# First attention of a three-block transformer: values as hi beside lo in one stationary operand, two products and a fold, and the queries' transposes at the head of a step

## The chip, the core and the metric

The kernel runs on one core of a Trainium2 chip. The core has five engines, each with its own queue that is worked off in order: TensorE (PE in the profile; its loads of the stationary operand are PEld), VectorE (DVE), ScalarE (ACT), GpSimd (POOL) and SyncE (SP), which only issues DMA transfers here. The metric is the device time of one execution in microseconds (us); lower is better. The times given are medians of a few runs.

## What is computed

Two small models run one after the other on a sequence of 256 tokens of width 1024. The first has two layers, of which the first is attention with 16 query heads of 64 in 4 key groups, over 256 context tokens and 256 own tokens; the second is a neighbourhood attention. The second model has two layers of attention, one dense feed-forward and one mixture of experts. All is float32. What matters here is the attention of the very first layer:

```python
def gqa_axial_mixer(hx, hc, w_in, q_g, k_g, w_out, cos, sin, need_ctx_out):
    px = hx @ w_in
    ...
    k_all = jnp.concatenate([kc, k], axis=1)
    v_all = jnp.concatenate([vc, v], axis=1)
    ...
    def block(qi):
        s = jnp.einsum('bqkgd,bskd->bkgqs', qi, k_all).astype(jnp.float32) * ATTN_SCALE
        p = jax.nn.softmax(s, axis=-1).astype(v_all.dtype)
        return jnp.einsum('bkgqs,bskd->bqkgd', p, v_all)

    o = lax.map(block, qb)
    o = o.transpose(1, 0, 2, 3, 4, 5).reshape(b, t, A_WIDTH)
    yx = (o * jax.nn.silu(z)) @ w_out
    ...
    sc = jnp.einsum('bqkgd,bskd->bkgqs', qc, kc).astype(jnp.float32) * ATTN_SCALE
    pc = jax.nn.softmax(sc, axis=-1).astype(vc.dtype)
    oc = jnp.einsum('bkgqs,bskd->bqkgd', pc, vc).reshape(b, lc, A_WIDTH)
    yc = (oc * jax.nn.silu(zc)) @ w_out
```

The own tokens look at all 512 keys, the context tokens at the 256 context keys.

## The kernel before, in words

TensorE multiplies a reduced-precision float type (fp32r). To come near float32, each operand is kept as two such numbers, hi (the rounded value) and lo (the rest), and a product is three matmuls into the same PSUM bank: hi by hi, hi by lo and lo by hi (`mm3`).

The first attention is worked off in 32 units: 4 key groups, in each the two sequences (own tokens with nk = 512 keys, then context with nk = 256), in each two tiles of 128 queries, and in each two pairs of heads (`pr` 0 and 1). `pipeline` runs steps i = -3 to 35; in step i it calls each stage of `stages0` for the unit that the stage's lag names, in the order of that list. This list is the only thing that sets the order, for every engine's queue is filled in the order in which the code is written. In step i the list holds, in this order: `pv` of unit i-4 (products of the weights with the values), `turn` of unit i-3 (transposes of the weights `e`), the normalisation of unit i-2 on GpSimd (`norm0`, `norm1`, after a reciprocal on VectorE), between them `back` of unit i-3 (the transposed weights `pt`: hi copied by ScalarE, lo by VectorE), `out` of unit i-4, `scores` of unit i, `soft` of unit i-1 (exponentials on ScalarE), `q_turn` of unit i+2, `peak` of unit i (maximum and its scaling on VectorE), `q_split` of unit i+3 and `fill`.

`q_split` and `q_turn` do something only for units of even number, since two units share a set of queries. `q_split` makes hi (ScalarE) and lo (GpSimd) of four heads beside each other in `qn`; it therefore falls into odd steps. `q_turn` transposes these four on TensorE into a PSUM bank and ScalarE copies them out (`qs`); it falls into even steps. The transposes of queries, of weights and of the modulation row share two PSUM banks (`tp`), which are given out in turn.

`fill` gives TensorE other work in each step. With r = i mod 8: for r = 0 to 3 two pieces of a modulation vector (products of 32x512, `wf` with `sc`), for r = 4 to 7 a quarter of the next group's gate projection (12 products of 128x512, `hh`, `hl` with `wh`, `wl`), and from step 28 on a part of the output projection. So one period of eight steps is one key group.

Values are held as `vd[0]` (hi) and `vd[1]` (lo), each with its 64 columns twice, so that a product with the values gives the same 64 rows twice, in partitions 0 to 63 and 64 to 127 of the bank `o` (of which there is one). `pv` does `mm3` for each tile of 128 keys, three matmuls with a moving operand of 256 columns (two heads of 128 queries). `out` then multiplies, per head, one half of the partitions by the gate z and 0.5 on VectorE (line 151, 64x128, into z itself), casts the result to `og` hi on VectorE (line 141, 128x128), and GpSimd makes `og` lo (line 144). The gate tile z is `zb` in the rows, the maximum and sums are `sm`, the scores `s`.

Lines in the profile are often those of small helpers: 130 `mm`, 138 `acopy`, 141 `vcopy`, 144 `tt`, 148 `ts`, 151 `stt`, 154 `gscale`, 160 `act`; 704 are the transposes of `q_turn`, 738 those of `turn`, 322 the modulation's products, 836 the maximum, 847 the reciprocal.

Of the kernel before, what the change touches and what calls it, by code (L numbers as in the profile page):

```python
# [7 lines left out]
F = mybir.dt.float32  # L8
R = mybir.dt.float32r
ACTF = mybir.ActivationFunctionType  # L10
ALU = mybir.AluOpType
# [89 lines left out]
def tile_net(  # L101
# [4 lines left out]
    nc = tc.nc  # L106
    ctx.enter_context(tc.manual_schedule())

    def pool(name, side="left", bufs=1, space=None):
        kw = {} if space is None else {"space": space}  # L110
        if space is None:
            kw["side"] = side
        return tc.tile_pool(name=name, bufs=bufs, reuse_waits="tile", **kw)
# [13 lines left out]
    def mm(o, l, r, start, stop, rows=None):  # L127

        pos = {} if rows is None else {"tile_position": (rows, 0)}
        nc.tensor.matmul(o, l, r, start=start, stop=stop, **pos)  # L130

    def mm3(o, l, r, start, stop, rows=None):
        mm(o, l[0], r[0], start, False, rows)
        mm(o, l[0], r[1], False, False, rows)
        mm(o, l[1], r[0], False, stop, rows)

    def acopy(o, i):
        nc.scalar.copy(out=o, in_=i)  # L138

    def vcopy(o, i):  # L140
        nc.vector.tensor_copy(out=o, in_=i)

    def tt(o, a, b, op, eng=None):
        (eng or nc.vector).tensor_tensor(out=o, in0=a, in1=b, op=op)  # L144
# [5 lines left out]
    def stt(o, a, s, b, op0, op1, eng=None):  # L150
        (eng or nc.vector).scalar_tensor_tensor(out=o, in0=a, scalar=s, in1=b, op0=op0, op1=op1)  # L151

    def gscale(o, i, s):
        nc.gpsimd.tensor_scalar(out=o, in0=i, scalar1=s, scalar2=1.0, op0=ALU.mult, op1=ALU.mult)  # L154

    def gsub_lo(lo, src, hi):
        tt(lo, src, hi.bitcast(F), ALU.subtract, nc.gpsimd)

    def act(o, i, f, **kw):
        nc.scalar.activation(out=o, in_=i, func=f, **kw)  # L160
# [85 lines left out]
    p0 = L0.enter_context(pool("l0"))  # L246
# [48 lines left out]
    def bank(tag="mm"):  # L295
        return (pmm if tag == "mm" else ptp).tile([128, 512], F, tag=tag, name=tag)
# [10 lines left out]
    p = bank("tp")  # L307
# [41 lines left out]
    for s, dst in ((0, xT), (1, cT)):  # L349
        for t in range(2):  # L350
            for half in range(2):
                ps = bank("tp")
# [3 lines left out]
                o = dst[:, 4 * half:4 * half + 4, t * 128:(t + 1) * 128]  # L356
                i = ps.rearrange("p (k n) -> p k n", k=4)
# [129 lines left out]
    def group_N(key, hh, hl, nt, ahead=0):  # L487


        pss = [bank() for _ in range(nt)]  # L490
        w = [ws.get(key) for _ in range(ahead)]
        if ahead:
            yield pss
        for ch in range(4):
            wh, wl = w.pop(0) if w else ws.get(key)
            for t in range(nt):
                sl = slice(t * 128, (t + 1) * 128)
                for k in range(2):
                    kt = 2 * ch + k
                    mm3(pss[t], (hh[:, kt, sl], hl[:, kt, sl]), (wh[:, k, :], wl[:, k, :]), kt == 0, kt == 7)  # L500
                yield pss
# [10 lines left out]

    qf = p0.tile([128, 4, D], F, name="qf")
    kk2 = [p0.tile([128, 4, 512], R, name=f"kk{i}") for i in range(2)]
    vd = [p0.tile([128, 4, 4, 2, 64], R, name=f"vd{i}") for i in range(2)]
    nm = Norm([xT, cT])
    for kt in range(KT):
        nm.add(kt)
# [32 lines left out]
    p = bank("tp")  # L551
# [50 lines left out]
    def heads(a):  # L602
        return a.rearrange("p (h d) -> p h d", d=64)
# [57 lines left out]
    def keys_split(t):  # L661

        src = heads(kf[:, t, :]).unsqueeze(2).to_broadcast([128, 4, 2, 64])
        kn[t] = [prope.tile([128, 4, 2, 64], R, tag=f"kn{i}", name=f"kn{i}", bufs=2) for i in range(2)]
        acopy(kn[t][0], src)
        tt(kn[t][1], src, kn[t][0].bitcast(F), ALU.subtract)

    def keys_turn(t):

        kp = (t + 2) % 4  # L670
        for part in range(2):
            ps = bank("tp")
            for g in range(4):
                nc.tensor.transpose(ps[:, g * 128:(g + 1) * 128],
                                    kn[t][part][:, g].rearrange("p a d -> p (a d)").bitcast(F), ident)
            acopy(kk2[part][:, :, kp * 128:(kp + 1) * 128], ps.rearrange("p (g n) -> p g n", g=4))
# [7 lines left out]
    class Unit0:  # L684
# [64 lines left out]
        def pv(self):  # L749
            nkt = self.nk // 128  # L750
            self.o = o = pop.tile([128, 2, 128], F, tag="o", name="o")
            for k in range(nkt):
                vt = (k + 2) % 4
                mm3(o.rearrange("p h n -> p (h n)"), [vd[i][:, vt, self.g].rearrange("p a d -> p (a d)") for i in range(2)],
                    [self.pt[i][:, k].rearrange("p h n -> p (h n)") for i in range(2)], k == 0, k == nkt - 1)

        def out(self):
            g, tok = self.g, slice(self.tt_ * 128, (self.tt_ + 1) * 128)
            z = zb[g][:, self.pr, tok]
            for h in range(2):  # L760
                sl = slice(h * 64, h * 64 + 64)
                stt(z[sl], self.o[sl, h, :], 0.5, z[sl], ALU.mult, ALU.mult)
            vcopy(og[g][0][:, self.pr, tok], z)
            gsub_lo(og[g][1][:, self.pr, tok], z, og[g][0][:, self.pr, tok])

# [7 lines left out]
    def l0_done(j, t, ps):  # L773
        if j == 0:
            acopy(kf[:, t, :], ps[:, 0:256])
            vsrc = heads(ps[:, 256:512]).unsqueeze(2).to_broadcast([128, 4, 2, 64])
            acopy(vd[0][:, t], vsrc)
            tt(vd[1][:, t], vsrc, vd[0][:, t].bitcast(F), ALU.subtract)
        else:
            acopy(qf[:, t, (j - 1) * 512:j * 512], ps)  # L780
        r = ropes[j]
        r.squares(t, ps)
        if j == 2 and t:
            if t >= 2:
                r.turn(t - 2)
            r.gain(t - 1)
            if t == 3:
                r.gain(3)
        if t == 3:
            roots, *rest = r.pieces(j == 2)  # L790
            if j == 0:
                for t_ in range(4):
                    rest.append(lambda t_=t_: keys_split(t_))
                    if t_:
                        rest.append(lambda t_=t_: keys_turn(t_ - 1))
                rest.append(lambda: keys_turn(3))
            if j == 1:
                for n in range(1):
                    rest += [units[2 * n].q_split, units[2 * n].q_turn]
            later[0:0] = [roots]  # L800
            later.extend(rest)

    proj_N("l0in", 3, hh, hl, 4, l0_done, 3, begun)

    def z_tile(g):
# [20 lines left out]
    pa = A0.enter_context(pool("att0", bufs=2))  # L826
# [18 lines left out]
    def soft_norm(st_, e, nk, h, on_act=False):  # L845
# [4 lines left out]
        else:  # L850
            gscale(e[:, h, 0:nk], e[:, h, 0:nk], st_[:, 3, h:h + 1])

    def pipeline(units, stages, fill=None):

        lags = [lag for f, lag in stages if f != "fill"]
        for i in range(min(0, min(lags)), len(units) + max(lags)):
            for f, lag in stages:
                if f == "fill":
                    fill(i + lag)
                elif 0 <= i - lag < len(units):  # L860
                    getattr(units[i - lag], f)()

    stages0 = (("pv", 4), ("turn", 3), ("norm0", 2), ("back", 3), ("norm1", 2), ("out", 4), ("scores", 0), ("soft", 1),
               ("q_turn", -2), ("peak", 0), ("q_split", -3), ("fill", 0))

    def mods():
        for a, b in ((0, 2), (1, 1), (1, 0), (1, 2)):
# [42 lines left out]
    def fill(i):  # L910


        if i == 28:
            for _ in mod:
                pass
        if i in {27: 1, 29: 2, 33: 3}:
            ws.split_to(ws.base + {27: 1, 29: 2, 33: 3}[i], nc.gpsimd)
        for a in out_steps.get(i, ()):
            out_step(*a)
        if i < 0 or i >= 28:  # L920
            return
        g, r = i // 8 + 1, i % 8
        if r < 4:
            next(mod)
            next(mod)
            if r == 3 and g < 4:
                zw["a"] = ws.get("l0z")
        elif g < 4:
            if r == 4:
                next(mod)  # L930
                zw["b"] = ws.get("l0z")
                zb[g] = z_tile(g)
            z_step(g, 2 * (r - 4))
            z_step(g, 2 * (r - 4) + 1)
        if i == 25:
            H.close()
            og.append([O.enter_context(pool("og3", "right")).tile([128, 2, 512], R, name=f"og3{i}") for i in range(2)])
# [130 lines left out]
    pa = A1.enter_context(pool("att1", "right", bufs=2))  # L1068
# [524 lines left out]
    for n in range(len(steps) + 1):  # L1593
        if n < len(steps):
            e, f = steps[n]
# [3 lines left out]
        if n:  # L1599
            e, f = steps[n - 1]  # L1600
# [214 lines left out]
    ps = bank("tp")  # L1815
# [155 lines left out]
    for n in range(len(steps) + 1):  # L1971
        if n < len(steps):
            e, f = steps[n]
# [11 lines left out]
        if n:  # L1985
            e, f = steps[n - 1]
# [62 lines left out]
    for t in range(2):  # L2049
        for d in range(2):  # L2050
            sl = slice(d * 512, d * 512 + 512)
# [86 lines left out]
```

## Time and profile before

| | us |
|---|---|
| median of 3 runs | 2044.96 (2042.16 to 2048.12) |
| the profiled execution | 2042.53 |
| its span, first to last instruction | 2040.8 |
| TensorE busy | 1957.9 (96%) |
| VectorE busy | 1601.8 (78%) |
| ScalarE busy | 1311.4 (64%) |
| GpSimd busy | 279.3 (14%) |

The first attention lies between about 126 and 288 us of the span. The busy times are sums over stages with different limits. A window gives each engine's busy time in a stretch; a row of the timeline is a run of like instructions on one engine, with its start, its length and, in brackets, how long the engine stood idle before it and what ended that. Matmuls overlap, so the distance between the starts of two rows tells more on TensorE than a row's length.

### The profile page before, as it was taken

To read this page: it belongs to the slowest core of one execution; us is meant where nothing else is said; L and a number is where in the kernel's file an instruction comes from. 1 tells how busy PE (TensorE), PEld (TensorE's weight loads), DVE (VectorE), ACT (ScalarE), POOL (GpSimd) and SP (SyncE) were. 2 spreads that over 40 slices of the span, in tenths; PEclk is the share of its full clock that TensorE was granted. 3 is DMA by queue.
4 is the path that set the end of the run, shared out by engine and by line. 5 is a ranking of instruction groups with operands and counts; after the bars stand their busy time and mean duration, and the time that the engine had idled before them with its cause. 6 is when DMAs were issued, how large, how long until landed. Compare 5 with 4: busy or idle time off the path is not lost. (4 is left out here: it accounts for less than half of the span.)

```text
span 2040.8 us, 29700 instructions
## 1 busy us (share of the span) xinstructions
PE 1957.9 (96%) x11046; PEld 1660.0 (81%) x11046; DVE 1601.8 (78%) x2100; ACT 1311.4 (64%) x1877; POOL 279.3 (14%) x365
## 2 busy tenths in 40 slices
PE   7999988999899899999989999999999999999997
PEld 3777777888888799998978888788878888788885
DVE  4676766358569876657779999999989999899997
ACT  3555543347657544445668777778777777777775
POOL 2123430005414311103420000000000000000000
PEclk9999998999999999999989999999999999999999
DMA  8333422444253256567659999899999999999990
GB/s 289 94 135 104 157 82 83 119 132 91 83 173 104 73 178 194 181 203 264 238 198 365 377 369 375 312 375 364 364 366 328 368 364 372 333 357 370 368 365 22
DMA packets 270327, 494.38 MB, mean 242 GB/s; under 512 B 22834, under 2 KB 108042, under 8 KB 270176
## 3 DMA queue, kind: packets, MB, share of 16 engines
q1 hardware_dynamic: 269312, 490.91, 69.0%
q8 instruction: 89, 1.46, 0.3%
q0 software_dynamic: 544, 0.98, 0.2%
q10 hardware_dynamic: 320, 0.53, 0.1%
q14 instruction: 62, 0.51, 0.1%
HBM read 491.29 MB, written 1.08 MB: 241 GB/s over the span
## 5 line engine op out<-in xcount | busy, mean ns | idle before, releaser
L86 DVE TENSOR_TENSOR wl<-w,wh 128x1024 fp32r<-128x1024 f32 x624 | 752.2, 1226 | 58.5 <-ACT wh L85 21.6
L85 ACT CAST wh<-w 128x1024 fp32r<-128x1024 f32 x626 | 652.6, 1052 | 144.1 <-PE mm L130 104.5
L130 PE MATMUL mm<-wh,X 128*128 128x512 f32 x1792 | 573.4, 393 | 0.0
L130 PEld LDWEIGHTS mm<-wh,X 128*128 128x128 f32 x1792 | 337.2, 188 | 69.2
L86 DVE TENSOR_TENSOR wl<-wf,wh 128x1024 fp32r<-128x1024 f32 x190 | 238.4, 1265 | 173.2 <-ACT wh L85 171.6
L130 PE MATMUL mm<-wl,X 128*128 128x512 f32 x896 | 349.5, 390 | 0.0
L85 ACT CAST wh<-wf 128x1024 fp32r<-128x1024 f32 x200 | 206.4, 1040 | 156.2 <-PE mm L130 131.6
L130 PE MATMUL y<-wh,hid 128*128 128x512 f32 x896 | 287.0, 390 | 0.7 <-ACT hid L138 0.7
L130 PEld LDWEIGHTS y<-wh,hid 128*128 128x128 f32 x896 | 168.1, 188 | 35.9 <-ACT hid L138 0.9
L130 PEld LDWEIGHTS mm<-wl,X 128*128 128x128 f32 x896 | 168.7, 188 | 33.7
L130 PE MATMUL y<-wl,hid 128*128 128x512 f32 x448 | 174.4, 389 | 0.0
L130 PE MATMUL mm<-hh,wh 128*128 128x256 f32 (+1 forms) x432 | 125.9, 292 | 5.1 <-ACT wh L85 3.2
L130 PE MATMUL mm<-hh,wl 128*128 128x256 f32 (+1 forms) x432 | 125.4, 290 | 1.4 <-DVE wl L86 1.3
L130 PE MATMUL mm<-hl,wh 128*128 128x256 f32 (+1 forms) x432 | 125.2, 290 | 0.0
L130 PEld LDWEIGHTS y<-wl,hid 128*128 128x128 f32 x448 | 84.1, 188 | 17.1
L130 PEld LDWEIGHTS mm<-hh,wh 128*128 128x128 f32 x432 | 83.2, 193 | 7.0 <-ACT wh L85 4.3
L130 PEld LDWEIGHTS mm<-hh,wl 128*128 128x128 f32 x432 | 83.2, 193 | 2.5 <-DVE wl L86 1.9
L154 POOL TENSOR_SCALAR e<-e,sm 128x512 f32<-128x512 f32 (+2 forms) x112 | 66.9, 608 | 124.7 <-DVE sm L847 114.4
L130 PEld LDWEIGHTS mm<-hl,wh 128*128 128x128 f32 x432 | 83.2, 193 | 0.6
L130 PE MATMUL fill<-hh,wh 128*128 128x256 f32 (+1 forms) x240 | 75.0, 313 | 1.2 <-DVE ev L144 0.7
L144 DVE TENSOR_TENSOR pt<-tp,pt 128x512 fp32r<-128x512 f32 (+2 forms) x80 | 41.5, 552 | 41.2 <-ACT pt L138 41.2
L160 ACT ACTIVATE e<-s,sm 128x512 f32<-128x512 f32 (+2 forms) x128 | 71.8, 571 | 2.4 <-DVE sm L148 1.5
(351 smaller groups left out, 3438.9 us busy)
## 6 DMA issues: line engine op xcount, KB each, us to landing
w<-in_e_w_dram SPq DMA_DIRECT2D x313, 1024.0 KB, 7.1
wf<-in_w_dram SPq DMA_DIRECT2D x64, 512.0 KB, 4.6
wf<-in_w_mod_dram SPq DMA_DIRECT2D x48, 512.0 KB, 4.6
wf<-in_w_qkv_dram SPq DMA_DIRECT2D x48, 512.0 KB, 4.6
xT<-in_e_w_dram SPq DMA_DIRECT2D x23, 1024.0 KB, 7.1
wf<-in_b_w_in_dram SPq DMA_DIRECT2D x32, 512.0 KB, 3.8
wf<-in_a_w_in_dram SPq DMA_DIRECT2D x20, 512.0 KB, 3.7
wf<-in_w_o_dram SPq DMA_DIRECT2D x16, 512.0 KB, 3.4
```

What stands on the lines that cost most here:

```text
L85: nc.scalar.copy(out=hi[:, 0:m], in_=src)
L86: (low or nc.vector).tensor_tensor(out=lo[:, 0:m], in0=src, in1=hi[:, 0:m].bitcast(F), op=ALU.subtract)
L130: nc.tensor.matmul(o, l, r, start=start, stop=stop, **pos)
L144: (eng or nc.vector).tensor_tensor(out=o, in0=a, in1=b, op=op)
L154: nc.gpsimd.tensor_scalar(out=o, in0=i, scalar1=s, scalar2=1.0, op0=ALU.mult, op1=ALU.mult)
L160: nc.scalar.activation(out=o, in_=i, func=f, **kw)
```

## The change

Three things are changed, all in the first attention.

The values lie in one tile `vd`: in each group 64 columns of hi and beside them 64 columns of lo. `pv` does two matmuls for a tile of keys (`mm2`): this operand with the weights' hi and with their lo. Partitions 0 to 63 of `o` then hold the hi part, 64 to 127 the lo part; the product of lo with lo comes in addition to the three of before.

A new function `fold` adds the two: ScalarE copies partitions 64 to 127 with a factor of 0.5 into `fu`, and VectorE multiplies partitions 0 to 63 by 0.5 and adds `fu`, once for each head, into the two halves of `ft`. `out` then multiplies by z on GpSimd, and the cast and the low part follow as before.

`q_turn` moves from behind `soft` to the head of the list of stages.

```diff
+    def mm2(o, l, r, start, stop):
+
+        mm(o, l, r[0], start, False)
+        mm(o, l, r[1], False, stop)
...
-    vd = [p0.tile([128, 4, 4, 2, 64], R, name=f"vd{i}") for i in range(2)]
+    vd = p0.tile([128, 4, 4, 2, 64], R, name="vd")
...
-                mm3(o.rearrange("p h n -> p (h n)"), [vd[i][:, vt, self.g].rearrange("p a d -> p (a d)") for i in range(2)],
+                mm2(o.rearrange("p h n -> p (h n)"), vd[:, vt, self.g].rearrange("p a d -> p (a d)"),
                     [self.pt[i][:, k].rearrange("p h n -> p (h n)") for i in range(2)], k == 0, k == nkt - 1)
...
-            for h in range(2):
-                sl = slice(h * 64, h * 64 + 64)
-                stt(z[sl], self.o[sl, h, :], 0.5, z[sl], ALU.mult, ALU.mult)
+            t = fold(self.o, 128)
+            tt(z, t, z, ALU.mult, nc.gpsimd)
             vcopy(og[g][0][:, self.pr, tok], z)
             gsub_lo(og[g][1][:, self.pr, tok], z, og[g][0][:, self.pr, tok])
...
-            vsrc = heads(ps[:, 256:512]).unsqueeze(2).to_broadcast([128, 4, 2, 64])
-            acopy(vd[0][:, t], vsrc)
-            tt(vd[1][:, t], vsrc, vd[0][:, t].bitcast(F), ALU.subtract)
+            vsrc = heads(ps[:, 256:512])
+            acopy(vd[:, t, :, 0, :], vsrc)
+            tt(vd[:, t, :, 1, :], vsrc, vd[:, t, :, 0, :].bitcast(F), ALU.subtract)
...
+    def fold(o, n):
+
+        u = pa.tile([64, 2, n], F, tag="fu", name="fu", bufs=2)
+        t = pa.tile([128, n], F, tag="ft", name="ft", bufs=2)
+        act(u, o[64:128], ACTF.Copy, scale=0.5)
+        for h in range(2):
+            stt(t[h * 64:h * 64 + 64], o[0:64, h, :], 0.5, u[:, h, :], ALU.mult, ALU.add)
+        return t
...
-    stages0 = (("pv", 4), ("turn", 3), ("norm0", 2), ("back", 3), ("norm1", 2), ("out", 4), ("scores", 0), ("soft", 1),
-               ("q_turn", -2), ("peak", 0), ("q_split", -3), ("fill", 0))
+    stages0 = (("q_turn", -2), ("pv", 4), ("turn", 3), ("norm0", 2), ("back", 3), ("norm1", 2), ("out", 4), ("scores", 0),
+               ("soft", 1), ("peak", 0), ("q_split", -3), ("fill", 0))
```

How the queues change is seen at two places. The first is TensorE's queue in step 18, an even step with modulation in its fill (`o` are the products with the values, `e` the weights, `s` the scores, `qn` the queries). Before:

```order
L130 MATMUL o<-pt_1566,vd_205 128x256
L130 MATMUL o<-pt_1567,vd_205 128x256
L130 MATMUL o<-pt_1566,vd_206 128x256
...
L738 MATMUL tp<-cs,e 128x128 x4
L130 MATMUL s_1625<-kk_203,qs 128x512
...
L704 MATMUL tp<-cs,qn 128x128 x4
L322 MATMUL fill<-wf,sc_141 32x512 x4
```

After, from the end of step 17 on:

```order
L327 MATMUL fill<-wf,sc_141 32x512 x4
L709 MATMUL tp<-cs,qn 128x128 x4
L130 MATMUL o<-pt_1565,vd 128x256
L130 MATMUL o<-pt_1566,vd 128x256
...
L743 MATMUL tp<-cs,e 128x128 x4
L130 MATMUL s_1637<-kk_203,qs 128x512
```

The transposes of queries stand right behind the fill of step 17 now, ahead of the products of step 18. Of these, left out above in part, there are four instead of six, two for each of two tiles of keys.

The second place is step 17, an odd one, on VectorE and on GpSimd, with what each instruction waits for (`ft` and `fu` are the fold's tiles, `og` the gated output, `zb` the gate). VectorE before:

```order
L144 TENSOR_TENSOR pt_1567<-tp,pt_1566 128x2x128 [waits Activation_49] x2
L151 SCALAR_TENSOR_TENSOR zb<-o,zb 64x128 x2
L141 CAST og_240<-zb 128x128 [waits DVE_49]
L836 TENSOR_REDUCE sm<-s_1577 128x2 [waits PE_49,Pool_49]
L148 TENSOR_SCALAR sm<-sm 128x2 [waits DVE_49]
```

VectorE after:

```order
L149 TENSOR_TENSOR pt_1566<-tp,pt_1565 128x2x128 [waits Activation_49] x2
L156 SCALAR_TENSOR_TENSOR ft<-o,fu 64x128 [waits Activation_49]
L156 SCALAR_TENSOR_TENSOR ft<-o,fu 64x128
L146 CAST og_239<-zb 128x128 [waits Pool_49]
L840 TENSOR_REDUCE sm<-s_1580 128x2 [waits PE_49]
```

GpSimd before, step 17 and the first instruction of step 18:

```order
L154 TENSOR_SCALAR e<-e,sm 128x256 [waits DVE_49,PE_49]
L154 TENSOR_SCALAR e<-e,sm 128x256 [waits Activation_49]
L144 TENSOR_TENSOR og_241<-zb,og_240 128x128 [waits DVE_49]
L144 TENSOR_TENSOR qn<-qf,qn 128x4x64 [waits PE_49,Activation_49]
L154 TENSOR_SCALAR e<-e,sm 128x512 [waits DVE_49]
```

GpSimd after:

```order
L159 TENSOR_SCALAR e<-e,sm 128x256 [waits DVE_49,PE_49]
L159 TENSOR_SCALAR e<-e,sm 128x256 [waits Activation_49]
L149 TENSOR_TENSOR zb<-ft,zb 128x128 [waits DVE_49]
L149 TENSOR_TENSOR og_240<-zb,og_239 128x128 [waits DVE_49]
L149 TENSOR_TENSOR qn<-qf,qn 128x4x64 [waits PE_49,Activation_49]
```
The product with the gate has moved from VectorE to GpSimd, ahead of `og` and `qn`, and VectorE's cast waits for GpSimd instead of VectorE's own product.

## Rows read from the trace of the kernel before

**Rows 1.** Windows: edges, length, busy us (PE, PEld, DVE, ACT, POOL), PEclk, DMA share.

```profile
60.00:110.00 50.00, 49.76 (x236) 41.24 (x235) 29.50 (x50) 24.68 (x46) 7.32 (x19) 1.00 0.31 95
176.84:189.81 12.97, 12.31 (x80) 11.02 (x81) 9.97 (x25) 7.74 (x18) 5.05 (x9) 1.00 0.52 168
189.81:201.67 11.86, 11.27 (x74) 10.09 (x73) 6.83 (x18) 5.05 (x15) 3.93 (x8) 1.00 0.01 2
201.67:208.60 6.93, 6.93 (x50) 4.28 (x48) 5.18 (x16) 4.79 (x15) 2.35 (x6) 1.00 0.29 92
208.60:216.37 7.77, 7.54 (x56) 4.85 (x53) 6.19 (x16) 5.28 (x15) 4.30 (x7) 1.00 0.92 316
```

**Rows 2.** Waits of PE, 113 to 290 us: us in total, times, longest us.

```profile
PE tp L704 <- DVE pt L144: 5.4, 7, 1.5
```

**Rows 3.** Timeline from 205.33: start us, us, engine, line, operation, out<-in [idle <-releaser].

```profile
205.33 0.98 PE L130 MATMUL o<-pt,vd 128*128 128x256 f32 x6
...
206.15 0.60 PE L738 MATMUL tp<-cs,e 128*128 128x128 f32 x4
...
206.57 0.65 ACT L138 CAST pt<-tp 128x256 fp32r<-128x256 f32 x2 [1.54 <-PE tp L738]
...
206.97 0.76 DVE L144 TENSOR_TENSOR pt<-tp,pt 128x256 fp32r<-128x256 f32 x2 [0.73 <-ACT pt L138]
...
207.65 0.58 DVE L151 SCALAR_TENSOR_TENSOR zb<-o,zb 64x128 f32<-64x128 f32 x2
...
208.26 0.23 DVE L141 CAST og<-zb 128x128 fp32r<-128x128 f32 x1
...
208.57 0.46 POOL L144 TENSOR_TENSOR og<-zb,og 128x128 fp32r<-128x128 f32 x1 [1.22 <-DVE og L141]
...
208.99 0.73 POOL L144 TENSOR_TENSOR qn<-qf,qn 128x256 fp32r<-128x256 f32 x1
...
209.86 0.16 DVE L847 RECIPROCAL sm<-sm 128x2 f32<-128x2 f32 x1
...
210.81 0.63 PE L704 MATMUL tp<-cs,qn 128*128 128x128 f32 x4
```

**Rows 4.** Timeline of other places, columns as in rows 3.

```profile
189.52 0.73 POOL L144 TENSOR_TENSOR qn<-qf,qn 128x256 fp32r<-128x256 f32 x1
...
193.34 0.63 PE L704 MATMUL tp<-cs,qn 128*128 128x128 f32 x4 [0.59 <-DVE pt L144]
...
200.84 0.74 POOL L144 TENSOR_TENSOR qn<-qf,qn 128x256 fp32r<-128x256 f32 x1
...
214.44 1.29 DVE L144 TENSOR_TENSOR pt<-tp,pt 128x512 fp32r<-128x512 f32 x2 [1.16 <-ACT pt L138]
...
216.37 1.66 PE L130 MATMUL o<-pt,vd 128*128 128x256 f32 x12 [0.23 <-ACT e L160]
...
216.99 0.75 POOL L144 TENSOR_TENSOR qn<-qf,qn 128x256 fp32r<-128x256 f32 x1
...
217.87 1.04 PE L738 MATMUL tp<-cs,e 128*128 128x128 f32 x8
...
219.16 0.16 DVE L847 RECIPROCAL sm<-sm 128x2 f32<-128x2 f32 x1
...
219.23 1.27 DVE L144 TENSOR_TENSOR pt<-tp,pt 128x512 fp32r<-128x512 f32 x2
```

**Rows 5.** Two tiles, whole span: duration ns min/median/max, first and last start.

```profile
L138 ACT CAST og<-o x16: 350/366/369, 631.8 to 693.2; 64x256 fp32r<-64x256 f32 x16
...
L144 POOL TENSOR_TENSOR og<-zb,og x32: 455/459/1367, 142.3 to 289.3; 128x128 fp32r<-128x128 f32 x32
```

**Rows 6.** Timeline, the first step of the attention.

```profile
126.33 1.20 PE L130 MATMUL s<-kk,qs 128*128 128x512 f32 x4 [0.73 <-DVE zb L151]
...
126.61 0.74 POOL L144 TENSOR_TENSOR qn<-qf,qn 128x256 fp32r<-128x256 f32 x1 [7.38 <-ACT qn L138]
```

**Rows 7.** One window later in the kernel, columns as in rows 1.

```profile
1030.00:1050.00 20.00, 15.06 (x76) 13.14 (x75) 15.48 (x29) 12.65 (x20) 7.92 (x3) 0.74 0.29 107
```

## The prediction

> **What bounds the kernel now.** Read first the windows of the attention of the first layer, two steps to a row [rows 1]. TensorE is busy for 12.31 of 12.97 us, 11.27 of 11.86, 6.93 of 6.93 and 7.54 of 7.77; VectorE for 6.19 of 7.77 where it is fullest, GpSimd there for 4.30. So TensorE sets the pace, and time can be won only on its queue, or lost by making that queue wait. The four rows are one period of eight steps, 39.5 us, of which the stage has three; the steps before the first period fill the pipeline, and eight come after the last, with one set of queries' transposes among them. Next, the waits of TensorE [rows 2]: 5.4 us go to the transposes of queries, seven times, for a PSUM bank. Then one stretch in order of time, with all engines [rows 3]. There the reader should see the way round of one step: TensorE's products with the values (o), the transposes of the weights e, ScalarE's copy of them (pt), VectorE's low part of them (pt), its two products with the gate (zb), the cast (og), and GpSimd's low parts of og and, in every second step, of the queries (qn). TensorE begins the next step at 208.60 (the edge between two windows of rows 1), while GpSimd ends qn only at 208.99 + 0.73 = 209.72. Nobody minds, since the transposes that read qn come at 210.81.
>
> **What the products give back.** Twelve products take 1.50 us until the next operation starts, six take 0.82 [rows 3, 4], so one costs (1.50 - 0.82)/6 = 0.113 us. Of 288, 96 go: 10.9 us, 0.45 in a step of 512 keys and 0.23 in one of 256. That is all that the change can win there, plus at most the 5.4 us of waits for the bank.
>
> **What the fold adds.** On ScalarE a scaled copy of 64x256 out of PSUM, 32 times, 0.37 each by the nearest row [rows 5]. It stands between the copies of pt and the exponentials; VectorE works meanwhile on the low parts. Three such copies from 206.57 on, at most 0.37 each, end 1.1 later, and VectorE comes to its next operation 207.65 - 206.57 = 1.08 after that start [rows 3]. So I take nothing for it; with the cover gone it is up to 0.37 a step. VectorE keeps two products of the same shape. New is that the product with the gate goes to GpSimd, and that VectorE's cast waits for it. Behind this wait are queued the maximum of the scores, its scaling, the reciprocal and the next low parts; GpSimd's own og and qn wait for the cast in turn. Its price: from VectorE to GpSimd 208.57 - (208.26 + 0.23) = 0.08, the same back, 0.46 for an operation of 128x128 (median of 32) [rows 3, 5], less the 0.03 that now lies between product and cast: 0.59 us in each step. The longest of those 32 took 1.37 [rows 5], which is the upper end; the lower end is zero, if the trip lay beside other work. I take 0.59, since VectorE stands still in that time and nothing else runs beside it there.
> The Trainium skill (SBUF — State Buffer, section "SBUF: two separate sides") says that VectorE and GpSimd lock a pair of ports against each other, for an operation of VectorE with two SBUF inputs too. By that rule the long row met such an operation, and the new one, which meets none, would be short.
>
> **What the moved transposes cost.** The code splits a query's four heads at the end of an odd step, with the low part (qn) last on GpSimd's queue, and now transposes them at the head of the next, even step. TensorE takes its matmuls in order, so no even step begins before qn is done. Before, 2.2 us of other work lay between. The loop that results, from transposes of queries to the next such transposes, for the pair from 201.67 to 208.60, by starts in rows 3:
> - transposes of queries 0.6 (a row of four, 0.63); four products 0.82 - 0.23 = 0.59; transposes of e until VectorE's low part 206.97 - 206.15 = 0.82. Sum 2.01.
> - from VectorE's low part to its next: the reciprocal of the next step starts 209.86 - 206.97 = 2.89 later, and a low part can follow 0.07 after it [rows 4]; plus the trip: 3.55. By TensorE alone it would be 208.60 - 206.15 + 0.59 = 3.04, so VectorE sets this.
> - from there to the end of qn 209.72 - 206.97 = 2.75, the trip 0.59, and 0.08 to TensorE: 3.42.
> In all 8.98 against 6.93: 2.05 lost. In the pair after it the second step has 512 keys in its low part: 2.01 + 3.55, then 216.99 + 0.75 - 214.44 = 3.30 [rows 4] and 0.67 again: 9.53 against 7.77, 1.76 lost.
> In the two pairs that also hold the projection of the gate, TensorE has more of its own to do, and qn ends at 189.52 + 0.73 = 190.25 and 200.84 + 0.74 = 201.58 [rows 4], 13.41 and 11.77 after the pair began. From these go 0.90 for eight products, and 0.67 comes on. In the first, the wait for the bank stays (the next transposes need the same one): 13.18 against 12.97, 0.21 lost. In the second it goes, 0.59 [rows 4]: 10.95 against 11.86, 0.91 won.
> One period loses 2.05 + 1.76 + 0.21 - 0.91 = 3.1, three of them 9.3.
> While the pipeline fills, the same wait stands three times: qn ends 1.0 us after the step's scores could start (126.61 + 0.74 against 126.33 [rows 6]), and two more like it. These add up, because the exponentials that ScalarE does ahead of each split hang on those scores: 3.0 lost. In the last eight steps 24 products go, 2.7 us; there VectorE's products hold the one bank of o, so I take half, 1.4 won, with 0 and 2.7 for the ends. The split of the values when they are made gets smaller on ScalarE and VectorE; TensorE is busy for 49.76 of 50 us there [rows 1], which hides it, and without that cover it would be a gain.
> Sum: 9.3 + 3.0 - 1.4 = 10.9 us slower. The profiled execution took 2042.53 (span 2040.8), so 2053.4; it lies 2.4 below the median of the runs, 2044.96, against which the sum gives 2055.9. The work after this stage begins when it ends and does not get shorter, so I pass the loss on in full.
>
> **Rivals.**
> *TensorE keeps its pace (faster).* If qn were done each time TensorE is, the pairs without the projection would run at VectorE's 3.55 a step, about as long as now, and the others would win 0.90 each and the wait of 0.59: 2.4 a period, 7.2, and 1.4 at the end. 8.6 less, 2036.4. It decides from the point where GpSimd ends qn 209.72 - 208.60 = 1.12 us earlier than now; with one operation more in its queue ahead of qn, that is against the order of the code.
> *The order costs, the fold does not.* If the trip to GpSimd lay beside other work, 2 x 0.59 go in the first pair, 0.67 in the second (where TensorE then is the later), 0.59 in each of the others: 3.0 of the 3.1. The start stays lost, the end won: 3 x 0.1 + 3.0 - 1.4 = 1.9, 2046.9. For it: GpSimd is busy for 15.6 of the 39.5 us only [rows 1]. Against it: the cast stands in VectorE's own order ahead of all the rest.
> *The fold costs more.* With 1.37 instead of 0.46 each of the six trips adds 0.91, in three periods 16 us: 2072.
> *TensorE's clock falls.* Granted was 1.00 in this stage, and 0.74 in a stretch where TensorE was busy for 15.06 of 20 us [rows 7]. In the pairs without the projection it would be busy for some 6.5 of 9.0 us, with stops of about two. At 1.2 in place of 2.4 GHz, 6.5 become 13.0, 4.0 more on each of six pairs: 2080. The stops in this stage so far, up to 1.5 us [rows 2], did not bring it down, so I hold it unlikely. The Trainium skill (TensorE: Matmul & The Clock Gate, section "HAM oscillation — how this bites in real kernels") warns that waits between short bursts of matmuls throttle the clock each time anew.
>
> **How the numbers follow.** A measurement of this kernel can tell about 0.3%, 6.1 us, from no change: faster is below 2038.8, slower above 2051.1. Chances: my forecast 0.60, TensorE's pace 0.11, the order alone 0.17, the dearer fold 0.07, the clock 0.05. The forecast's own spread (the trip between 0.45 and 0.75, the start, the end) is 2049 to 2062, a tenth of it below 2051.1. Slower: 0.54 + 0.12 = 0.66. Same: 0.06, the order alone, less a little of it on either side: 0.22. Faster: 0.12. The range from 2044 to 2064 holds the forecast, the order alone, and part of the dearer fold, 0.8 in all.
>
> **What would show it.** In the windows of the stage the pairs without the projection take 9.0 and 9.5 us, and TensorE's share in them falls to some 70%; the list of waits names the transposes of queries behind GpSimd, about two us in each of these pairs. VectorE's cast waits 0.6 for GpSimd, and 192 products are left. The order step is wrong if these pairs stay below 8 us; the trip is wrong if the cast waits much less or more; and if the granted clock of the stage is below 1.00, the loss is the clock's.

## The result, and the profile after

| | median, us | runs |
|---|---|---|
| before, measured beside it | 2045.22 (2041.42 to 2049.04) | 6 |
| after | 2055.73 (2053.00 to 2059.68) | 6 |

The ratio is 1.0054, with a 95% interval from 1.0042 to 1.0067: about 11 us slower. The profiled execution of after took 2057.76 us, its span is 2055.9, 15.1 more than before's.

The windows of one period, cut at the queries' transposes, columns as in rows 1. The four rows answer to the last four of [rows 1], in the same order:

```profile
144.51:157.28 12.77, 11.43 (x73) 9.88 (x73) 8.98 (x23) 8.37 (x19) 5.25 (x9) 1.00 0.50 171
157.28:167.96 10.68, 10.32 (x64) 8.98 (x64) 6.15 (x17) 5.74 (x17) 4.42 (x9) 1.00 0.00 1
167.96:176.58 8.62, 6.72 (x44) 3.86 (x44) 6.34 (x18) 5.79 (x17) 4.39 (x9) 1.00 0.42 144
176.58:185.89 9.31, 7.16 (x48) 4.30 (x49) 6.35 (x17) 7.58 (x18) 5.24 (x9) 1.00 0.68 230
```

TensorE, busy for 6.93 of 6.93 us before, is busy for 6.72 of 8.62 in the third row. In the two rows without the projection no other engine is fuller than 7.58 of 9.31: no engine's own work is the bound there, a chain of waits is. Which one, TensorE's two longest waits in this stage say (113 to 310 us; columns as in rows 2):

```profile
PE tp L709 <- POOL qn L149: 19.9, 15, 2.2
PE s L130 <- POOL wl L86: 1.9, 1, 1.9
```

The queries' transposes no longer wait 5.4 us for the bank [rows 2]; of that kind 1.5 us are left in the whole stage, at the transposes of the modulation row. Instead the queries' transposes wait 15 times for qn, 19.9 us in all. One round of that chain, in order of time, of all engines, columns as in rows 3 (a number in brackets is the idle time ahead of the instruction, and what ended it; ... stands for rows left out):

```profile
167.96 0.66 PE L709 MATMUL tp<-cs,qn 128*128 128x128 f32 x4 [0.36 <-POOL qn L149]
...
168.38 0.72 PE L130 MATMUL o<-pt,vd 128*128 128x256 f32 x4
...
169.76 0.85 DVE L149 TENSOR_TENSOR pt<-tp,pt 128x256 fp32r<-128x256 f32 x2 [0.73 <-ACT pt L143]
170.17 0.38 ACT L165 ACTIVATE fu<-o 64x256 f32<-64x256 f32 x1
...
170.59 0.58 DVE L156 SCALAR_TENSOR_TENSOR ft<-o,fu 64x128 f32<-64x128 f32 x2
...
171.25 0.46 POOL L149 TENSOR_TENSOR zb<-ft,zb 128x128 f32<-128x128 f32 x1 [1.11 <-DVE ft L156]
...
171.74 0.23 DVE L146 CAST og<-zb 128x128 fp32r<-128x128 f32 x1 [0.58 <-POOL zb L149]
171.89 1.22 DVE L840 TENSOR_REDUCE sm<-s 128x2 f32<-128x1024 f32 x1
...
173.22 0.16 DVE L851 RECIPROCAL sm<-sm 128x2 f32<-128x2 f32 x1
...
173.29 0.73 DVE L149 TENSOR_TENSOR pt<-tp,pt 128x256 fp32r<-128x256 f32 x2
...
175.09 0.23 DVE L146 CAST og<-zb 128x128 fp32r<-128x128 f32 x1 [0.57 <-POOL zb L149]
...
175.80 0.72 POOL L149 TENSOR_TENSOR qn<-qf,qn 128x256 fp32r<-128x256 f32 x1
...
176.58 0.66 PE L709 MATMUL tp<-cs,qn 128*128 128x128 f32 x4 [1.90 <-POOL qn L149]
177.00 0.72 PE L130 MATMUL o<-pt,vd 128*128 128x256 f32 x4
```

Follow it by the starts: transposes at 167.96, products at 168.38, VectorE's low part at 169.76, its two adds (the fold) at 170.59, GpSimd's product with the gate at 171.25, VectorE's cast at 171.74 after 0.58 idle, the maximum at 171.89, the next low part at 173.29, the same once more, and qn at 175.80, whose end releases the transposes at 176.58. TensorE stands still for 1.90 us there.

Where the time went is read from two marks: the last matmul of the part ahead of the attention, and the first and last product with the values. The rows are that matmul in the timelines of before and of after, then the tile o of before and of after (count: shortest/median/longest ns, first to last start):

```profile
125.21 0.39 PE L130 MATMUL mm<-hh,wl 128*128 128x512 f32 x1
```

```profile
129.81 0.39 PE L130 MATMUL mm<-hh,wl 128*128 128x512 f32 x1
```

```profile
L130 PE MATMUL o<-pt,vd x288: 274/283/387, 137.2 to 288.0; 128*128 128x256 f32 x144
```

```profile
L130 PE MATMUL o<-pt,vd x192: 274/283/415, 144.9 to 302.0; 128*128 128x256 f32 x192
```

From 125.21 to 288.0 are 162.8 us, from 129.81 to 302.0 are 172.2: the stage took 9.4 more. 4.6 of the 15.1 came before it (129.81 - 125.21), and what is left of the spans behind it is 2040.8 - 288.0 = 1752.8 and 2055.9 - 302.0 = 1753.9. TensorE's instructions in the part ahead are the same 498 matmuls in both, yet they keep it busy for 114.75 us in after and 110.78 in before, at a mean granted clock of 0.93 against 0.99. In the executions profiled for the experiments this matmul starts between 125.53 and 128.25 us, at 0.95 to 0.97, and in a second one of the changed kernel at 127.33, at 0.95. So this start varies from execution to execution, by 2.5 us between two of the changed kernel; of the thirteen profiled, before's happens to be the quickest and after's the slowest, and no run ties the 4.6 us to the change. From here on "stage" is the length from that matmul to the last product's start, in one profiled execution.

### The profile page after: what moved, and what is told of

It is laid out like the page before. It is cut to its first block, busy times and chain, and to the rows that moved or that the text cites. A ratio compares the mean times of both kernels' runs of the same rounds, so it can differ in the third digit from the quotient of the medians.

```text
span 2055.9 us, 29533 instructions
## 1 busy us (share of the span) xinstructions
PE 1954.9 (95%) x10950; PEld 1652.3 (80%) x10950; DVE 1598.6 (78%) x2100; ACT 1326.7 (65%) x1909; POOL 293.9 (14%) x397
## 5 line engine op out<-in xcount | busy, mean ns | idle before, releaser
L130 PE MATMUL fill<-hh,wl 128*128 128x256 f32 (+1 forms) x240 | 72.9, 304 | 0.0
```

## The experiments

All ratios are against the kernel before, run on the same chip in the same session, with 95% intervals; before's medians there were 2043.45 to 2045.63. 0.001 is 2.04 us.

### The two halves apart

The fold and the two products, with the old order:

```diff
-    stages0 = (("q_turn", -2), ("pv", 4), ("turn", 3), ("norm0", 2), ("back", 3), ("norm1", 2), ("out", 4), ("scores", 0),
-               ("soft", 1), ("peak", 0), ("q_split", -3), ("fill", 0))
+    stages0 = (("pv", 4), ("turn", 3), ("norm0", 2), ("back", 3), ("norm1", 2), ("out", 4), ("scores", 0), ("soft", 1),
+               ("q_turn", -2), ("peak", 0), ("q_split", -3), ("fill", 0))
```

> The changed kernel with the old order of the stages: two products and the fold, but the queries' transposes behind the exponentials as before. My theory (the loss comes from the transposes that wait for qn at the head of even steps; the fold by itself is cheap): 192 products, no wait of TensorE for qn above 0.5 us, the pairs of steps with modulation at 7.0 and 7.7 us (VectorE's 3.55 a step), the pairs with the gate's projection 0.9 shorter than before; about 6 us faster than before, near 2039. Rival (the fold's way over ScalarE, VectorE and GpSimd costs by itself): the kernel is no faster than before, pairs with modulation of 7.5 us or more, 2045 to 2051.

Measured: 2041.39, ratio 0.9987 (0.9978 to 0.9997), stage 158.0. A gain, smaller by the ratio than expected. TensorE's list of waits has none for qn there; the waits of the queries' transposes for the bank are 7.8 us, ten times, where they were 5.4, seven times.

The new order alone, with three products and no fold (that change of the list made to the kernel before):

> The kernel before with only the move of the queries' transposes to the head of the step; three products and the gate on VectorE as before. My theory: the wait for qn arises here too, since qn ended about 1.1 us after the next step's start already; pairs with modulation of about 8.3 and 9.2 us against 6.9 and 7.8, waits of TensorE for qn of some 15 us in all, the kernel about 10 us slower than before, near 2055. Rival (the move costs only together with the fold's trip to GpSimd): within 3 us of before, 2042 to 2048.

Measured: 2052.12, ratio 1.0045 (1.0031 to 1.0059), stage 170.1. From its list of waits (columns as in rows 2), TensorE's longest:

```profile
PE tp L704 <- POOL qn L144: 13.2, 12, 1.8
```

So the order alone makes most of the loss, 9 us by the ratio (6 to 12 by its interval) and 7.3 by the stage, and the wait for qn is there without any fold. Its four windows, cut at the queries' transposes as above, are 13.21, 11.12, 8.06 and 9.06, together 41.45 for 39.53 before: at full clock the whole loss of a period comes from the order, for the changed kernel's first period is 41.38. With the products changed as well, the wait for qn grows from 13.2 to 19.9 us: what TensorE no longer does, it waits. What gains 2.7 us in the old order loses 1.9 in the new one (1.0054 against 1.0045; by the intervals anything from a gain of 2 to a loss of 6), and TensorE's clock, which fell in after and not here, is enough for that (2.4 us, below).

### Where qn is made

If the chain through qn is the cause, making qn early must turn the loss round. In the changed kernel, the split of the queries is put first in a step:

```diff
-    stages0 = (("q_turn", -2), ("pv", 4), ("turn", 3), ("norm0", 2), ("back", 3), ("norm1", 2), ("out", 4), ("scores", 0),
-               ("soft", 1), ("peak", 0), ("q_split", -3), ("fill", 0))
+    stages0 = (("q_split", -3), ("q_turn", -2), ("pv", 4), ("turn", 3), ("norm0", 2), ("back", 3), ("norm1", 2), ("out", 4),
+               ("scores", 0), ("soft", 1), ("peak", 0), ("fill", 0))
```

> The changed kernel with the split of the queries at the head of its odd step, so that qn stands on ScalarE's and GpSimd's queues ahead of the rest of that step; transposes at the head of the next step, fold and two products as in the change. My theory: the waits for qn go but for the first one while the pipeline fills; pairs with modulation at VectorE's pace, 7.0 and 7.7 us, those with the projection 1.5 us shorter than before each; about 6 us faster than before, 2039. Rival (the wait is for the PSUM bank or for VectorE, and qn is only the name that the profile gives): the pairs stay above 8 us, 2050 or more.

Measured: 2037.40, ratio 0.9973 (0.9962 to 0.9985), stage 153.7, by the two ratios some 17 us faster than the changed kernel, for two instructions moved (ScalarE's and GpSimd's halves of the split). In its list of waits one of the 15 for qn is left, in the first step:

```profile
PE tp L709 <- POOL qn L149: 1.8, 1, 1.8
```

Is it qn alone, or do the early transposes have a part in it? With the split first and the transposes back behind the exponentials:

> The changed kernel with the queries' split first in a step and the queries' transposes back at their old place behind the exponentials. Theory: once qn is early, the early transposes are worth something by themselves, since they do not stand behind the bank of the values' transposes: the old place brings the bank wait back (1.7 us in 10 places of the kernel with the old order), and the time is near that of the old order, 2040 to 2042. Rival: all that counts is that qn is early, and the time is that of split first with the transposes first, 2036 to 2038.

Measured: 2041.57, ratio 0.9985 (0.9977 to 0.9994), as with the old order altogether (0.9987). In its list of waits TensorE's longest is the one for the bank, as in [rows 2] and in the old order's 7.8 us (the 1.7 of the expectation is the longest of those ten):

```profile
PE tp L709 <- DVE pt L149: 7.2, 7, 2.0
```

So the early transposes do bring something, the end of the bank wait, but only with an early qn; and the early split alone brings nothing that these times can tell.

Last, the kernel before with both moved and its three products kept:

> The kernel before with the queries' split first in a step and the queries' transposes second, and nothing else changed: three products, no fold. It completes the table of three orders (old; transposes first; split and transposes first) with and without the change of the products. Theory that the order's gain and the products' gain add: split first with three products and the fold stands at a ratio of 1.0002 to the kernel before, the fold's own price is 3.3 us, so this is at 0.9986, 2041. Rival, that the order only helps where the fold is: the time of the kernel before, 2043 to 2046.

Measured: 2040.84, ratio 0.9982 (0.9973 to 0.9991), stage 158.6. The order with both moved gains by itself, fold or not.

### What a product and the fold are worth

The old order and the fold, with three products for a tile of keys (the second done twice):

```diff
         mm(o, l, r[0], start, False)
-        mm(o, l, r[1], False, stop)
+        mm(o, l, r[1], False, False)
+        mm(o, l, r[1], False, stop)
```

> The old order with the fold and the new values' form, but three products for a tile of keys (the second is done twice, so that TensorE works as long as in the kernel before; the output is not the reference's). It takes the fold's price apart from what the 96 removed products bring; the old order with fold and two products stood at a ratio of 0.9987 to the kernel before. By the prediction's price of one product (0.113 us, 96 of them 10.9 if TensorE sets the pace in all steps) this is 2052, and the fold cost some 8. If only the steps that TensorE bounds (half of them) feel the products, it is 2046 to 2048 and the fold cost 2 to 3 (taken). If the products lay beside other work everywhere, it is 2041 to 2043, as with two, and the fold cost nothing.

Measured: 2047.75, ratio 1.0016 (1.0007 to 1.0025). The same edit with the split first:

> The changed kernel with the queries' split first in a step, and three products as above (the output is not the reference's). Here TensorE hardly waits (2.5 and 1.8 us of waits for the queries in the whole stage), so the 96 products should cost near their full 10.9 us over split first with two products (ratio 0.9973, some 2038): 2047 to 2049 (taken). If they lie beside VectorE's fold even so, 2041 to 2044.

Measured: 2044.91, ratio 1.0002 (0.9993 to 1.0010), below what I took. All in one table:

| order of the step | three products, no fold | three products and fold | two products and fold |
|---|---|---|---|
| old | 1 | 1.0016 | 0.9987 |
| transposes first | 1.0045 | | 1.0054 (1.0055 again) |
| split and transposes first | 0.9982 | 1.0002 | 0.9973 |

By rows, the 96 products are worth 0.0029 both times, 5.9 us, not 10.9. The fold costs 0.0016 and 0.0020, 3.3 and 4.1 us. Each of these differences is uncertain by some 2.7 us, by the two intervals that it is taken from, but both rows agree. The stages of the profiled executions put the products a little higher (6.8 and 7.4 us: 164.8 against 158.0, 161.2 against 153.7) and the fold a little lower (2.0 and 2.5). Why the products bring half to two thirds shows in the windows of one period with the split first, cut at the queries' transposes as above, with two products, then with three:

```profile
151.61:161.72 10.11, 10.11 (x65) 9.07 (x64) 6.76 (x19) 5.90 (x17) 4.70 (x10) 1.00 0.00 1
161.72:168.43 6.71, 6.58 (x46) 3.80 (x44) 4.92 (x15) 5.50 (x16) 3.51 (x8) 1.00 0.28 74
168.43:175.57 7.14, 7.07 (x52) 4.28 (x48) 5.74 (x16) 6.15 (x17) 5.16 (x9) 1.00 0.97 325
175.57:188.13 12.56, 11.47 (x76) 10.00 (x73) 10.04 (x25) 9.24 (x22) 6.02 (x12) 1.00 0.61 196
```

```profile
153.72:164.79 11.07, 11.07 (x73) 10.02 (x72) 6.75 (x19) 5.90 (x17) 4.69 (x10) 1.00 0.01 2
164.79:171.75 6.96, 6.96 (x50) 4.28 (x48) 4.79 (x15) 5.42 (x16) 3.75 (x8) 1.00 0.29 87
171.75:179.16 7.41, 7.41 (x56) 4.77 (x52) 6.07 (x16) 6.08 (x17) 4.99 (x9) 1.00 0.95 306
179.16:192.07 12.91, 12.43 (x85) 10.96 (x82) 10.04 (x25) 9.29 (x22) 5.96 (x11) 1.00 0.58 185
```

In the first row of each, eight products at 0.113 us, 0.90 in all, come back in full: 11.07 - 10.11 = 0.96. In the last row, of the same eight, 12.91 - 12.56 = 0.35; in the middle ones, of 0.45 each, 0.25 and 0.27. TensorE is busy for the whole first window and for 11.47 of 12.56 in the last: where it was already waiting, a shorter queue only waits longer. In a period 1.83 of 2.71 come back.

### The trip to GpSimd

In the changed kernel, the product with the gate on VectorE:

```diff
-            tt(z, t, z, ALU.mult, nc.gpsimd)
+            tt(z, t, z, ALU.mult)
```

> The changed kernel with the product with the gate on VectorE instead of GpSimd; all else as in the change. My theory: the trip to GpSimd (0.57 us between VectorE's product and its cast) becomes an operation of some 0.25 us; in the loop there are six such trips in a period of eight steps, so 0.3 x 6 x 3 = 5 us less than the changed kernel, near 2050, with TensorE's waits for qn still about 15 us. Rival (the trip is free, as GpSimd and VectorE have time): the same time as the changed kernel, 2055.

Measured: 2050.83, ratio 1.0037 (1.0026 to 1.0047): 3.5 us under the changed kernel, about as much as the intervals leave open. The profile is clearer: from the first product of one period to that of the next, in the first period and at full clock in both, it is 40.4 instead of 41.4. So the trip lies on the path of the changed kernel. The same edit with the split first:

> Split first, transposes first, and the gating product z = z * t on VectorE in place of GpSimd. The trip from VectorE to GpSimd and back (0.57 to 0.60 us of VectorE's idleness a step) becomes an operation of 0.29 on VectorE itself. Where VectorE sets the pace, all 32 steps, that is 0.28 to 0.31 a step or up to 9 us: 2028. Where the trip was overlapped or TensorE sets the pace (the steps without mod), half the steps count: 2033 (taken). Rival: VectorE's idleness in the trip cost nothing because TensorE sets the pace now: 2037 as without it.

Measured: 2035.20, ratio 0.9955 (0.9942 to 0.9968), the fastest of all: 9 us under the kernel before and 22 under the changed one beside it. How much of it is the trip is less sure than the time itself. The stage became only 0.8 us shorter (152.9 against 153.7); the other 2.9 of the 3.7 between 0.9973 and 0.9955 lie within the two intervals. There the rival fits, that TensorE sets the pace and the trip lies mostly beside its work.

### TensorE's clock

In the profile of after, TensorE's granted clock falls in places (0.72 from 218 to 224 us, 0.75 from 230 to 236). The changed kernel once more, unchanged, and then with work for TensorE where it waits:

> The changed kernel once more, unchanged, beside the next three. If the clock that TensorE was granted between 216 and 306 us of its first profiled execution (0.66 to 0.81 in places) belongs to this order of work, its new profile shows windows under 0.9 in the mod steps again; if it was an accident of one execution, 1.00 throughout. Time 2053 to 2057 either way. The stage from its first step to the last product should be 8 to 10 us longer than the kernel before's 161.9, and the 4.6 us that the stretch ahead of it took longer should vary from execution to execution, since its instructions are the same.

Measured: 2056.92, ratio 1.0055 (1.0043 to 1.0067). The clock fell again, in more places. One stretch, first of after, then of after again (columns as in rows 1):

```profile
212.00:236.00 24.00, 19.96 (x115) 13.54 (x115) 15.12 (x38) 15.93 (x39) 10.99 (x20) 0.86 0.58 198
```

```profile
212.00:236.00 24.00, 19.86 (x113) 14.43 (x114) 15.66 (x41) 15.10 (x35) 10.49 (x19) 0.86 0.60 198
```

The stage took 176.1 us, not 8 to 10 but 13 longer than before's, while the part ahead took 127.3: that one does vary by itself.

Then eight extra products, whose results nobody reads, ahead of every second set of the queries' transposes:

```diff
                 ps = tbank()
+                for i in range(8 if self.s else 0):
+                    mm(ps, kk2[0][:, 0, 0:128], kk2[1][:, 0, 0:512], True, True)
                 for h in range(4):
```

> The changed kernel with eight extra products of 512 columns (results thrown away) on TensorE ahead of the queries' transposes in every second pair, the mod pairs, where it waits 1.9 to 2.15 us for qn. At some 0.22 us each they fill about 1.8 us of each wait. Theory that the clock falls because TensorE stops there (loss 1.56 + 1.0 + 1.3, some 4 us): the windows return to 1.00 and the time falls by 2 to 4 us, to 2052 to 2053.5, though more work is done. Rival, that the clock has another cause: the windows stay low, and the time stays at 2055.5 or rises by up to 2 us.

Measured: 2053.97, ratio 1.0053 (1.0040 to 1.0066). The median is 3 lower than that of the unchanged kernel beside it, the ratios are the same: the times don't decide. The profile does. The same stretch, then the third and fourth window of a period:

```profile
212.00:236.00 24.00, 23.38 (x146) 17.09 (x145) 17.21 (x45) 17.18 (x41) 11.47 (x21) 1.00 0.68 217
```

```profile
166.07:174.71 8.64, 8.64 (x53) 5.30 (x53) 6.35 (x18) 5.76 (x17) 4.39 (x9) 1.00 0.45 136
174.71:184.04 9.33, 9.20 (x57) 5.72 (x56) 6.35 (x17) 7.60 (x18) 5.25 (x9) 1.00 0.73 235
```

The clock is 1.00 throughout, and the two windows are as long as in after (8.62 and 9.31) with TensorE now busy in nearly all of them: it was never the bound there. The three periods take 41.4 us each, 124.3 in all. In after they take 126.7, in its second execution 129.6. So the clock cost 2.4 and 5.3 us in the periods of those two executions. That is one profiled execution of warm, the fastest of its five; of the others only the mean clock of the whole execution is known, 0.984 to 0.988, where the changed kernel's twelve have 0.982 to 0.988, so whether the clock stayed up in them too is open. That warm is not faster by as much has one more reason in sight: in the first two places, while the pipeline fills, the eight extra products take longer than the wait they fill (1.04 and 1.26 us), and the pipeline's start gets 1.4 us longer (16.5 instead of 15.1).

## Why the prediction was right, and where it was not

Forecast were 2055.9 us, slower, with 10.9 lost; measured were 2055.73 and 10.5. The direction holds, and so does the cause, the wait for a late qn, as the order alone and the split put first show. The sum is better than its terms.

- *What bounds the kernel.* Right: the waits of TensorE decide. The order step too: 8.62 and 9.31 in the pairs without the projection, where 8.98 and 9.53 were forecast, and TensorE's share in them 78 and 77%, where I said some 70.
- *The chain of a pair.* Forecast as 2.01 + 3.55 + 3.42, measured as 1.80 + 3.53 + 3.29. Of the 0.21 in the first part 0.18 are one misreading: I took the length of the transposes' row, some 0.6 us, as the time until the products start, and they start 0.42 after them (176.58 to 177.00), since matmuls overlap. Starts to starts, as for the other steps, would have been right.
- *The pairs with the projection.* Forecast 13.18 and 10.95, measured 12.77 and 10.68; the first lost nothing against its 12.97. Without the fold's terms and with all products the forecast's figures would be 13.41 + 0.08 = 13.49 and 11.77 + 0.08 - 0.59 = 11.26; the kernel with the order alone takes 13.21 and 11.12. So 0.28 and 0.14 of the misses are in the order's part. Fold and products together then bring 0.44 in each (13.21 to 12.77, 11.12 to 10.68), where the forecast had 0.90 - 0.59 = 0.31.
- *The trip's length* was right: VectorE's cast waits 0.57 or 0.58 us, and the sum over the stage, 19.2 us for 32 of them, is 0.60 each:

```profile
DVE og L146 <- POOL zb L149: 19.2, 32, 1.3
```

- *The trip's price* was a little less than its length. Ahead of the cast it adds 0.54: from VectorE's two operations on `o` to the cast are 1.15 us (170.59 to 171.74), before 0.61 (207.65 to 208.26 [rows 3]). But the maximum follows the cast 0.15 later, before 0.26:

```profile
208.52 1.22 DVE L836 TENSOR_REDUCE sm<-s 128x2 f32<-128x1024 f32 x1
```

  So on VectorE's own way it adds 0.43 (1.30 against 0.87), not 0.59. That the step came out at 3.53 for 3.55 is therefore luck: in this even step the low parts took 0.15 longer until the adds (0.83 against 0.68). Nor does every trip lie on the path. With the product on VectorE the cast comes 0.21 earlier (0.94 after the adds), and the four windows are 0.20, 0.21, 0.33 and 0.22 shorter, 0.96 in all: between four and five of the eight trips of a period lie on the path, where I charged six.
- *The fold's copy on ScalarE* was put at nothing. That was right but for one wait of VectorE for it, 2.0 us, in the last step.
- *The period* grew by 1.85 us (41.38 against 39.53), not 3.1. Of the 1.26 too much, 0.68 are in the pairs with the projection, some 0.4 the transposes' misreading in the two others.
- *The products* were put at 10.9 us at the most. With the rest unchanged they bring 5.9 by the ratios, and the prediction did not say how much would come back; it let them count in full in the pairs with the projection.
- *The start* was right: 3.0 us were forecast for it, and the first product comes 15.1 us after the part ahead (144.92 - 129.81) where it came after 12.0 (137.19 - 125.21). *The end* was right in its size only: the last eight steps took 1.7 less (30.4 us, 271.6 to 302.0, against 32.1, 255.9 to 288.0), where 1.4 was forecast for 24 products saved. But the kernel with the order alone, which saves none, takes 1.4 less there too (30.7, 267.1 to 297.8), and the old order with two products only 0.8 (31.3, 252.2 to 283.5). What the order takes away there is before's longest wait for the bank, 1.5 us [rows 2], ahead of the transposes at 260.46.
- *The clock* made up most of the difference, and I had held its fall unlikely (0.05) because stops of up to 1.5 us had not brought it down. The stops became 1.90 and 2.15, and it fell. The sum by the rows, with the clock at full, is 5.5 (three periods, 124.3 for 118.8) + 3.1 - 1.7 = 6.9; 2.4 of clock in the profiled execution bring it to 9.3, against the 9.4 that the stage lost. My 2080 for this rival let every pair without the projection run at half clock throughout; it ran so in parts of some of them only.

The two misses are of opposite sign: the pairs too dear by some 3.8 us in three periods, the clock left out with 2.4 to 5.3. That the total fits to 0.4 us is luck; that it is a loss of this size is not, since the order alone, without trip or a fall of the clock, loses 9 by the ratio and 7.3 by the stage.

Of the Trainium skill's two rules that the prediction named, the one on the clock (TensorE: Matmul & The Clock Gate, section "HAM oscillation — how this bites in real kernels"), that waits between short bursts of matmuls throttle it, is borne out by after's rows of 0.86 and warm's of 1.00; "each time anew" is not, as the first period ran at 1.00 with the same waits. The one on ports (SBUF — State Buffer, section "SBUF: two separate sides") fits the new operation, which meets no operation of VectorE: 465 ns at the most in 32 (the tile zb of after, columns as in rows 5). The longest of GpSimd's low parts of og still takes 1.37 us, beside an operation of VectorE that reads two tiles from SBUF (timeline of after):

```profile
L149 POOL TENSOR_TENSOR zb<-ft,zb x32: 455/460/465, 149.1 to 303.5; 128x128 f32<-128x128 f32 x32
```

```profile
304.19 1.22 DVE L86 TENSOR_TENSOR wl<-wf,wh 128x1024 fp32r<-128x1024 f32 x1
304.35 1.37 POOL L149 TENSOR_TENSOR og<-zb,og 128x128 fp32r<-128x128 f32 x1 [0.34 <-DVE og L146]
```

## What to carry to other kernels

An operation that is moved to the head of a step takes the making of its operand with it: look who writes what it reads, where that stands in its own engine's queue, and move that first. Here the same early transposes lose 9 us behind a late qn and gain 4 with an early one. The work that an edit takes from the bounding engine counts only in the windows where that engine has no waits; here half to two thirds of it came back.

## What the runs showed of the chip

TensorE's clock fell in this stage where stops of 1.9 to 2.2 us come twice in a period. In the kernel with the new order alone, stops of 1.1 and 1.6 us at the same places left it at 1.00 throughout; with the gate's product on VectorE they were 1.6 and 1.9, and it fell to 0.72 in three stretches of 6 us. A single stop of 1.8 us at the start of the stage left it at 1.00 in every kernel with the early transposes. It also did not fall in every period, nor in the same places in two executions of one kernel, so part of the scatter of such a kernel is likely the clock's. What it does is plain in the timeline of after, four products of the scores of one shape, first in the step before, then after a stop of 1.90:

```profile
213.91 1.17 PE L130 MATMUL s<-kk,qs 128*128 128x512 f32 x4
...
219.63 2.06 PE L130 MATMUL s<-kk,qs 128*128 128x512 f32 x4
```

The granted clock is 1.00 over the first row and 0.50 over the second (219.60 to 221.70), which is the lower of the two levels, 1.2 for 2.4 GHz; the four take 1.76 times as long.
